# Attention's softmax sums spread over partitions through DRAM, in place of a transpose and selector matmuls, for six of eight groups

## The chip, the core and the metric

The kernel runs on one core of a Trainium2 chip. The core has five engines that run their own instruction streams: TensorE (PE, matrix products; PEld is its weight load), VectorE (DVE), ScalarE (ACT), GpSimd (POOL) and SyncE (SP). In this kernel SP issues almost all DMA transfers, one after the other in one stream. Each engine takes its instructions in order, so an instruction that waits holds up all that stand behind it on that engine. The metric is the device time of one execution in microseconds (us), lower is better.

## The reference

One layer of a hybrid model over 1024 latent tokens (a grid of 16 rows of 64 columns, width 1024) with 256 context tokens: a norm, one projection into an attention part and a state-space part (SSD), both concatenated and projected out, then a gated MLP and a final norm. The change lies in the attention part, cut here to what matters:

```python
# per head (8 heads of 64): local window keys and all context keys in one softmax
scores = jnp.concatenate([s_loc.reshape(bsz, nh, GRID_W, n_loc), s_ctx], axis=-1)
p = jax.nn.softmax(scores.astype(jnp.float32), axis=-1)
out = einsum(p_loc, v_win) + einsum(p_ctx, v_ctx)
```

The softmax is computed as exponentials, their sum for each query and head, the product of the exponentials with v, and last a division of that product by the sum.

## The kernel before, in words

Attention is done in 64 steps (`steps`), one for each head pair `hp` (4), half of the grid's rows `rb` (2), column block `cb` (4) and head of the pair `j` (2). Eight steps with the same `hp` and `rb` are a group; the groups are numbered 0 to 7 here. A step has 128 queries and 640 keys. It goes through three functions, in a software pipeline written out by hand (the loop at L760): `attn_score(n)`, `attn_turn(n - 2)`, `attn_out(n - 3)` (for even steps) and one step of `work`, a generator that first carries the SSD chunks (`ssd_chunk`) and then the first half of the output projection (`out_steps`).

- `attn_score`: scores into PSUM (tile s, tag "big", three buffers of two banks), VectorE subtracts from the bias table `tabt` and takes the extreme (L627), ScalarE takes the exponential and adds it up along the keys into one column of `sm` (L628). So after eight steps `sm` is a tile of 128 queries (partitions) by 8 columns, one for each `cb` and `j`. This function also issues the loads of the next bias table half (`load_tab`, L597), of the next group's q and k (`load_qk`, L544 to L548) and of v (L583).
- `attn_turn`: five transposes of the exponentials (tile pt), copied to SBUF by ScalarE (pts, L639).
- `attn_out`: 20 matmul instructions into `av` (L655), a PSUM tile of one bank with one buffer, that holds for a whole group the output channels of two heads (128 partitions) by 512 queries.

The sums lie with the queries on partitions, and `av` has the queries along the row and the two heads' channels on partitions. So at the end of a group (n % 8 == 6) the reciprocals of the sums must be turned and spread over 64 partitions for each head. The kernel before does this on TensorE: a transpose of `sm` to 8 x 128 (L661, tile smt), a copy (L663, tile st), and four matmuls with selector matrices `selh` (L666, tile rp, eight instructions in the trace) that leave the reciprocals spread over 128 x 512 in PSUM. ScalarE copies them to `ao` (L671), VectorE multiplies `av` by `ao` into `ao` (L672). smt and rp share the PSUM tag "s1" (one bank, one buffer) with the SSD chunks' tiles cb, st, yd and later with ytp and the output projection's os and oa. Groups 0 to 4 are then stored to `a_d` in DRAM (L677) and read back later; groups 5 to 7 are split into two parts for the projection at once (`split_attn`, L684 and L685).

The order of instructions on each engine comes from a scheduler that looks at the code's order and at its own estimate of when each is ready; the code's order is a priority, not the order on the engine.

Of the SSD chunk, the loads `seg<-cum_d` (L439) are of interest: each spreads eight rows of 128 numbers over all 128 partitions by a DMA from DRAM. POOL waits for them at L440, VectorE behind POOL at L443, ScalarE behind VectorE at L444.

Of the kernel before, what the change touches and what calls it, by code (L numbers as in the profile page):

```python
# [10 lines left out]
FP = mybir.dt.float32  # L11
FR = mybir.dt.float32r
AF = mybir.ActivationFunctionType
OP = mybir.AluOpType
# [3 lines left out]
P = 128  # L18
# [18 lines left out]
def hymba(ctx: ExitStack, tc: tile.TileContext, A):  # L37
    nc = tc.nc
    act, dve, pool, pe, sp = nc.scalar, nc.vector, nc.gpsimd, nc.tensor, nc.sync

    const = ctx.enter_context(tc.tile_pool(name="const", bufs=1))
    dram = ctx.enter_context(tc.tile_pool(name="dram", bufs=1, space=DRAM))

    def f32(ap):
        return ap.bitcast(FP)
# [11 lines left out]
    mge, mle, mlt, mgt, ident, ones = (cst[:, i, :] for i in range(6))  # L57
# [5 lines left out]
    a_d = dram.tile([512, T], FP, name="a_d")  # L63
    cum_d = dram.tile([P, P], FP, name="cum_d")
    x1_d = dram.tile([P, KT, T], FP, name="x1_d")
    g_d = dram.tile([NF, P, T], FP, name="g_d")

    wpool = ctx.enter_context(tc.tile_pool(name="wpool", bufs=3, reuse_waits="tile"))

# [33 lines left out]
            pe.matmul(rb[:, t * P:e * P], ones, dg[:, t:e], start=True, stop=True)  # L103
        return rb

    # ---------------------------------------------------------------- projections
    pa = ExitStack()
    hx = pa.enter_context(tc.tile_pool(name="hx", reuse_waits="tile", bufs=1))
    pc = ExitStack()
# [10 lines left out]
    with ExitStack() as p0:  # L120
# [60 lines left out]
        for i in range(4):  # L181
# [10 lines left out]
            for h in range(2):  # L192
                if i == 0 and h:
                    rstd_rows(mmp, wk0, stats(wk0, xh[1], 4, "x1"), 4, "mm", "x1", "sqa4", rb=rbx[1])
                for kt in (2 * i, 2 * i + 1):
                    c = slice(512 * h, 512 * h + 512)
# [32 lines left out]
    with ExitStack() as p1:  # L229
# [40 lines left out]
        for blk in range(4):  # L270
# [3 lines left out]
            g = blk % 2  # L274
# [12 lines left out]
            s = 0.125 if isq else 1.0  # L287
# [35 lines left out]
    sd = ExitStack()  # L323
    ssd = sd.enter_context(tc.tile_pool(name="ssd", reuse_waits="tile", bufs=1, side="right"))
    dtp = sd.enter_context(tc.tile_pool(name="dtp", reuse_waits="tile", bufs=1, side="right"))
    # dt, decays and cumulative sums, tokens on partitions
    dtv = dtp.tile([P, 10, 16], FP, name="dtv")
    dta = dtp.tile([P, 10, 16], FP, name="dta")
    dtt = ExitStack()
# [239 lines left out]

    pa.close()  # L570

    # ---------------------------------------------------------------- attention and SSD
    pb = ExitStack()
    at = pb.enter_context(tc.tile_pool(name="at", reuse_waits="tile", bufs=2))
    bigp = pb.enter_context(tc.tile_pool(name="bigp", reuse_waits="tile", bufs=3, space=PSUM))
    onep = pb.enter_context(tc.tile_pool(name="onep", reuse_waits="tile", bufs=1, space=PSUM))
# [9 lines left out]
    selh = at.tile([8, 4, P], FP, name="selh", bufs=1)  # L586
# [16 lines left out]
    live = {}  # L603
# [40 lines left out]
    def attn_out(n):  # L644
        hp, rb, cb, _ = steps[n]
        vp = vps[hp]
        if n % 8 == 0:
            av_t[0] = onep.tile([P, 4, P], FP, tag="av", name=f"av{n}")
        av = av_t[0]
        pp = [live.pop(n), live.pop(n + 1)]  # L650
        for i in range(5):
            for j in range(2):
                key = i - 2 * j
                vt = vp[:, 4 * cb + rb + key if 0 <= key < 3 else 16 + (i - 3 if key > 2 else i), 64 * j:64 * j + 64]
                pe.matmul(av[64 * j:64 * j + 64, cb], vt, pp[j][:, i * P:(i + 1) * P],  # L655
                          start=i == 0, stop=i == 4, skip_group_check=True)
        if n % 8 == 6:
            sm = live.pop(("sums", n // 8))
            dve.reciprocal(sm, sm)
            sp_ = onep.tile([8, P], FP, tag="s1", name=f"smt{n}")  # L660
            pe.transpose(sp_, sm, ident)  # L661
            st = at.tile([8, P], FP, tag="st", name=f"st{n}", bufs=1)
            dve.tensor_copy(st, sp_)  # L663
            rp = onep.tile([P, 4, P], FP, tag="s1", name=f"rp{n}")
            for cb in range(4):
                pe.matmul(rp[:, cb], selh[:, cb], st,  # L666
                          start=True, stop=True)
            ao = at.tile([P, 8, 4, 16], FP, tag="ao", name=f"ao{n}", bufs=1)
            g4 = lambda ap: ap.rearrange("p b (r c) -> p b r c", r=8)
            av4 = ao.rearrange("p r b c -> p b r c")  # L670
            act.activation(av4, g4(rp), AF.Copy)  # L671
            dve.tensor_tensor(av4, g4(av), av4, OP.mult)  # L672
            ao = ao.rearrange("p r b c -> p (r b c)")
            if (0, rb) in out:
                split_attn(rb, hp, ao)
            else:
                sp.dma_start(a_d[hp * P:(hp + 1) * P, 512 * rb:512 * rb + 512], ao)  # L677
                out["stored"].append((rb, hp))

    out = {"stored": []}  # L680

    def split_attn(hf_, k, src):
        h, l = (o[:, k] for o in out[0, hf_])
        act.activation(h, src, AF.Copy)  # L684
        dve.tensor_tensor(l, src, f32(h), OP.subtract)  # L685
# [74 lines left out]
    for n in range(len(steps) + 3):  # L760
        out["n"] = n
        if n < 64:
            attn_score(n)
        if 0 <= n - 2 < 64:
            attn_turn(n - 2)
        if 0 <= n - 3 < 64 and (n - 3) % 2 == 0:
            attn_out(n - 3)
        next(work, None)
# [1 line left out]
        pass  # L770
    pb.close()

    # ---------------------------------------------------------------- output projection, second half
    psp = ctx.enter_context(tc.tile_pool(name="psp", reuse_waits="tile", bufs=8, space=PSUM))

    def bank(name, n=512):
# [19 lines left out]
            for o, i in ((4, 0), (4, 2), (5, 0), (5, 2), (6, 0), (6, 2), (3, 2))]  # L796
    yzf = yz.rearrange("p a b -> p (a b)")

    # the gated MLP's first product in seven block products of half the size (Strassen)
    ORDER = ((0, 4), (1, 1), (2, 2), (3, 0), (4, 3), (5, 0), (6, 3))  # L800

    B_SUMS = (((0, 0),), ((1, 0), (0, 0), OP.subtract), ((1, 1),), ((0, 0), (1, 1), OP.add),
# [96 lines left out]
    def norm2(hf_, which):  # L899
        c = slice(512 * hf_, 512 * hf_ + 512)  # L900
        rb = rms_rows((ssum[hf_],), wk, f"f{hf_}", yz[:, 0].rearrange("p (n t) -> p n t", n=4))
        yield
        rb = rb()
        for kt in range(KT):
            dve.scalar_tensor_tensor(xa[:, kt, c], xa[:, kt, c], scl[:, 2, kt:kt + 1], rb, OP.mult, OP.mult)
            act.activation(xa[:, kt, c], xa[:, kt, c], AF.Identity, bias=mod[:, 24 + kt:25 + kt])
            if kt % 2:
                yield
        for o in which:
            b_ops(hf_, (o,))  # L910
            yield

    attn_in(1)
    first = norm2(0, range(5))
# [11 lines left out]
    b_ops(0, (5, 6))  # L926
    second = norm2(1, range(7))

    # ---------------------------------------------------------------- gated MLP
    def g_load(hf_, k):  # L930
        h, l = gslots[k - 8]
        sp.dma_start(f32(l), g_d[k, :, 512 * hf_:512 * hf_ + 512])
        act.activation(h, f32(l), AF.Copy)
        dve.tensor_tensor(l, f32(l), f32(h), OP.subtract)
# [3 lines left out]
    for n, u in enumerate(passes):  # L938
        last = n + 1 == len(passes)
        bk = [bank(f"u{n}_{i}") for i in range(5)]  # L940
        r = [xa[:, (4 if units[u][1] else 0) + i] for i in range(2)]
        for o, t0, t1 in (parts[0], parts[0][:6] + parts[1][:6] + whole[6:], parts[1])[n] if n < 3 else whole:
            j = ORDER[o][1]
# [18 lines left out]
        if n == 2:  # L962
            finish(0, [xa[:, i] for i in range(2)])
            u, r = 1, [xa[:, 4 + i] for i in range(2)]
# [2 lines left out]
    g_load(0, 20)  # L967
    g_load(0, 21)

    # ---------------------------------------------------------------- down projection and final norm  # L970
    # of its 22 blocks along the sum, 8 go by the same seven block products and 14 directly
    mt4 = yz[:, 4:6].rearrange("p a (b t) -> p (a b) t", b=2)
    m1, m4, m5, m45 = (mt4[:, i] for i in range(4))
    srow = [yz[:, 6], ssum[1]]
# [62 lines left out]
    for hf_ in range(2):  # L1037
        c = slice(512 * hf_, 512 * hf_ + 512)
# [5 lines left out]
        for p in range(KT // 2):  # L1044
            first = hf_ == 1 and p == 3
# [9 lines left out]
            for i in range(2):  # L1055
                f = 2 * p + i
# [104 lines left out]
```

## Time and profile before

| what | value |
|---|---|
| timed runs | 1433.61, 1435.97 and 1436.22 us; median 1435.97 us |
| the profiled execution, first to last instruction (its span) | 1432.0 us |
| median of the timed runs above that span | 4.0 us |
| instructions in the profile | 19634 |
| TensorE busy | 1344.9 us, 94% of the span |
| VectorE, ScalarE, GpSimd busy | 955.2 us (67%), 598.9 us (42%), 583.6 us (41%) |
| attention's stretch | about 395 to 645 us |

The profiled execution's own time is known from its first to its last instruction, 1432.0 us; what lies before and after is not in the trace. Busy time is when an engine works on an instruction; the busy time of TensorE is modelled for pipelined matmuls, so close to full means that it rarely stands still, not that it is at its peak.

### The profile page before, as it was taken

Reading aid. Unit: us, or ns where it says so; the run is one execution under the profiler, and the core shown is the slowest. Engines: PE = TensorE matmul, PEld = TensorE weight load, DVE = VectorE, ACT = ScalarE, POOL = GpSimd, SP = SyncE. Lnnn points to the kernel's source line nnn. Section 1 sums busy time; section 2 is a strip of 40 time slices with the busy share of each in tenths; the row PEclk is TensorE's granted clock in tenths of the full one; section 3 lists DMA queues with packets and bytes.
Section 4 is the critical chain, followed back from the end, with each engine's and each line's share of the span. In section 5 each row is a group of like instructions: output and inputs, shape, how many; then the busy total and the mean of one; then the engine's idle time right before and its main releaser. Section 6 shows DMA issues by size and latency. Waiting matters only on the chain.

```text
span 1432.0 us, 19634 instructions
## 1 busy us (share of the span) xinstructions
PE 1344.9 (94%) x7539; PEld 1126.8 (79%) x7539; DVE 955.2 (67%) x1251; ACT 598.9 (42%) x987; POOL 583.6 (41%) x389
## 2 busy tenths in 40 slices
PE   5999899999989998999889999999999989998996
PEld 3788888889868787778777777777778767887885
DVE  5797434232367766548989777777787796488574
ACT  5432124342155558535535333344343443354331
POOL 0020000013657852014565676666676554334250
PEclk8999999999989999999989999999999999999998
DMA  9578862021697787343213222212222464364342
GB/s 372 213 238 233 245 228 77 30 74 38 181 253 204 208 222 256 100 153 111 74 48 115 74 89 74 60 73 88 89 88 89 134 224 140 107 199 125 107 141 74
DMA packets 86909, 202.23 MB, mean 141 GB/s; under 512 B 8472, under 2 KB 33816, under 8 KB 85536
## 3 DMA queue, kind: packets, MB, share of 16 engines
q1 hardware_dynamic: 83648, 189.45, 42.3%
q0 software_dynamic: 3168, 11.54, 2.0%
q8 instruction: 59, 0.97, 0.3%
q14 instruction: 34, 0.28, 0.1%
HBM read 163.40 MB, written 37.55 MB: 140 GB/s over the span
## 4 chain that ended last, share of the span: by engine, by line
PE 65%; DVE 15%; DMA 8%; issue 4%; ACT 3%; POOL 3%; SPq 2%; DVEq 0%; ACTq 0%; POOLq 0%
PE u L856 23%; PE pd L88 8%; PE fu_x L88 6%; PE pm L1010 3%; PE av L655 2%; PE tu_z L88 2%; PE oc L88 2%; PE tu_v L88 2%; DMA adal<-in_ada_wt 2%; PE os L88 2%; DMA seg<-cum_d 2%; PE pt L637 2%; PE oa L88 2%; PE s L616 1%; DVE wlu L849 1%
## 5 line engine op out<-in xcount | busy, mean ns | idle before, releaser
L856 PE MATMUL u<-op,whu 128*128 128x512 f32 (+1 forms) x760 | 229.7, 386 | 5.9 <-ACT whu L848 2.5
L856 PEld LDWEIGHTS u<-op,whu 128*128 128x128 f32 x760 | 141.9, 192 | 38.0 <-ACT whu L848 2.7
L856 PE MATMUL u<-op,wlu 128*128 128x512 f32 (+1 forms) x380 | 145.9, 385 | 2.2 <-DVE wlu L849 2.2
L849 DVE TENSOR_TENSOR wlu<-yz,whu 128x512 fp32r<-128x512 f32 x115 | 135.9, 1196 | 17.5 <-ACT whu L848 16.8
L847 POOL TENSOR_TENSOR yz<-as,as 128x512 f32<-128x512 f32 x69 | 118.9, 1735 | 46.7 <-DVE wlu L849 45.8
L848 ACT ACTIVATE whu<-yz 128x512 fp32r<-128x512 f32 x115 | 70.9, 626 | 116.1 <-PE u L856 68.0
L856 PE MATMUL u<-opx,whu 128*128 128x512 f32 (+1 forms) x384 | 113.1, 383 | 3.5 <-ACT whu L848 3.5
L395 POOL TENSOR_TENSOR xwc<-ctm,wendc 128x512 f32<-128x512 f32 x4 | 4.7, 1166 | 218.6 <-PE fu_c L88 200.9
L847 POOL TENSOR_TENSOR yz<-as 128x512 f32<-128x512 f32 x46 | 64.0, 1400 | 62.1 <-DVE wlu L849 52.4
L856 PEld LDWEIGHTS u<-opx,whu 128*128 128x128 f32 x384 | 69.6, 191 | 22.2 <-ACT whu L848 8.9
L856 PEld LDWEIGHTS u<-op,wlu 128*128 128x128 f32 x380 | 73.0, 192 | 17.6 <-DVE wlu L849 2.6
L88 PE MATMUL pd<-opx,wh_dn 128*128 128x512 f32 x256 | 80.6, 398 | 3.7 <-ACT wh_dn L77 3.7
L856 PE MATMUL u<-opx,wlu 128*128 128x512 f32 (+1 forms) x192 | 72.7, 380 | 0.0
L887 POOL TENSOR_TENSOR xa<-xa 128x1024 f32<-128x1024 f32 x20 | 51.7, 2586 | 45.6 <-DVE xa L877 45.4
L628 ACT ACTIVATE pr<-pr,mx 128x640 f32<-128x640 f32 x64 | 52.8, 826 | 40.5 <-DVE mx L627 40.4
L627 DVE CUSTOM_DVE_ANT_0 pr<-s,tabt 128x640 f32<-128x640 f32 x64 | 52.0, 818 | 20.6 <-PE s L617 15.8
L849 DVE TENSOR_TENSOR wlu<-as,whu 128x512 fp32r<-128x512 f32 x46 | 46.2, 1004 | 26.0 <-ACT whu L848 26.0
L655 PE MATMUL av<-pts,vp 128*64 128x128 f32 x640 | 56.4, 289 | 5.5 <-ACT pts L639 4.9
L208 DVE CUSTOM_DVE_ANT_0 adal<-adal,crow 128x1024 f32<-128x1024 f32 x32 | 39.6, 1240 | 30.8 <-DMA adal<-in_ada_wt 30.8
L88 PEld LDWEIGHTS pd<-opx,wh_dn 128*128 128x128 f32 x256 | 47.5, 188 | 16.0 <-ACT wh_dn L77 4.8
L856 PE MATMUL u<-opz,whu 128*128 128x512 f32 (+1 forms) x192 | 57.4, 381 | 0.6 <-DVE opz L816 0.6
L639 ACT ACTIVATE pts<-pt 128x640 f32<-128x640 f32 x64 | 43.8, 696 | 32.2 <-PE pt L637 20.3
(660 smaller groups left out, 3785.5 us busy)
## 6 DMA issues: line engine op xcount, KB each, us to landing
as<-in_w_up SPq DMA_DIRECT2D x46, 512.0 KB, 4.2
adal<-in_ada_wt SPq DMA_DIRECT2D x32, 512.0 KB, 4.7
ws_dn<-in_w_down SPq DMA_DIRECT2D x32, 448.0 KB, 3.5
g_d<-xa POOLq DMA_DIRECT2D x22, 512.0 KB, 4.5
tabt<-in_tab SPq DMA_DIRECT2D x48, 192.0 KB, 4.4
adaw<-in_ada_w SPq DMA_DIRECT2D x8, 1024.0 KB, 12.2
seg<-cum_d SPq DMA_DIRECT2D x16, 512.0 KB, 5.5
q<-q_d SPq DMA_DIRECT2D x32, 256.0 KB, 6.5
```

What stands on the lines that cost most here:

```text
L88: pe.matmul(out[:, t0:t1], st(a, k), mv(b, k, t0, t1), start=k == 0 and p == 0, stop=k == kend - 1 and p == 2, **kw)
L208: dve.tensor_tensor_reduce(w, w, crow, 1.0, 0.0, OP.mult, OP.add, modr[:, f - 16:f - 15])
L627: dve.tensor_tensor_reduce(pr, ps[:, lo:lo + 640], tabt[m % 2][:, 384 * j:384 * j + 640], -1.0, BIG, OP.add, OP.min, mx)
L628: act.activation(pr, pr, AF.Exp, bias=mx, scale=-1.0, accum_out=sm[:, n % 8:n % 8 + 1])
L639: act.activation(pts, pt[:, 0:640], AF.Copy)
L655: pe.matmul(av[64 * j:64 * j + 64, cb], vt, pp[j][:, i * P:(i + 1) * P], start=i == 0, stop=i == 4, skip_group_check=True)
L847: pool.tensor_tensor(src, e[0], e[1], e[2])
L848: act.activation(h, src, AF.Copy)
L849: dve.tensor_tensor(l, src, f32(h), OP.subtract)
L856: pe.matmul(ps[:, t0:t1], aops[n, o][a][:, k], bops[o][b][:, k, t0:t1], start=first and o < 5 and (t0 == 0 or n == 2), stop=end, skip_grou ...
L887: (dve if p == 0 else pool).tensor_tensor(r[i], r[i], tmp, OP.mult)
L1010: pe.matmul(dst[o], aops[n, o][a][:, k], sops[o][b][:, k], start=k == i == 0 and (o in (0, 2, 4) or o > 4 and first), stop=k == 3 and i == ...
```

## The change

For groups 0 to 5 the reciprocals go to DRAM and come back spread. A DRAM tensor `s_d` (6 x 8 x 128) is added. At the end of such a group SP stores `sm` (128 partitions of 8 numbers) into it turned, so that each of the 8 columns becomes a row of 128; in DRAM neighbouring numbers of one partition then lie 512 bytes apart. Two loads follow, one for each head of the pair, that read four rows of 128 numbers and repeat them over 64 partitions, into a new SBUF tile `rows` (128 x 512, one buffer). ScalarE copies `av` itself from PSUM to `ao`. The product of `ao` and `rows` on VectorE (`normalised`) is written later in the code: after the next group's first 20 `av` matmuls. What follows the product (the store to `a_d`, or the split) moves with it. Groups 6 and 7 keep the old way. The rest of the diff only takes away comments.

```diff
+    s_d = dram.tile([6, 8, P], FP, name="s_d")
...
+        if n % 8 == 0 and "rows" in live:
+            normalised(*live.pop("rows"))
         if n % 8 == 6:
-            sm = live.pop(("sums", n // 8))
+            g = n // 8
+            sm = live.pop(("sums", g))
             dve.reciprocal(sm, sm)
-            sp_ = onep.tile([8, P], FP, tag="s1", name=f"smt{n}")
-            pe.transpose(sp_, sm, ident)
-            st = at.tile([8, P], FP, tag="st", name=f"st{n}", bufs=1)
-            dve.tensor_copy(st, sp_)
-            rp = onep.tile([P, 4, P], FP, tag="s1", name=f"rp{n}")
-            for cb in range(4):
-                pe.matmul(rp[:, cb], selh[:, cb], st,
-                          start=True, stop=True)
             ao = at.tile([P, 8, 4, 16], FP, tag="ao", name=f"ao{n}", bufs=1)
-            g4 = lambda ap: ap.rearrange("p b (r c) -> p b r c", r=8)
             av4 = ao.rearrange("p r b c -> p b r c")
-            act.activation(av4, g4(rp), AF.Copy)
-            dve.tensor_tensor(av4, g4(av), av4, OP.mult)
...
+            if g < 6:
+                rows = at.tile([P, 4, P], FP, tag="rows", name=f"rows{n}", bufs=1)
+                sp.dma_start(s_d[g].rearrange("k q -> q k"), sm)
+                for j in range(2):
+                    src = s_d[g].rearrange("(b j) q -> j b q", j=2)[j]
+                    sp.dma_start(rows[64 * j:64 * j + 64], src.partition_broadcast(64))
+                act.activation(av4, g4(av), AF.Copy)
+                live["rows"] = (ao, rows, hp, rb)
             else:
...
+                act.activation(av4, g4(rp), AF.Copy)
+                dve.tensor_tensor(av4, g4(av), av4, OP.mult)
+                attn_done(ao, hp, rb)
...
+    def normalised(ao, rows, hp, rb):
+        av4 = ao.rearrange("p r b c -> p b r c")
+        dve.tensor_tensor(av4, av4, g4(rows), OP.mult)
+        attn_done(ao, hp, rb)
+
+    def attn_done(ao, hp, rb):
+        ao = ao.rearrange("p r b c -> p (r b c)")
+        if (0, rb) in out:
+            split_attn(rb, hp, ao)
+        else:
+            sp.dma_start(a_d[hp * P:(hp + 1) * P, 512 * rb:512 * rb + 512], ao)
+            out["stored"].append((rb, hp))
```

## Rows read from the trace of the kernel before

**Rows 1.** The page: busy time, share of the span, instructions of each engine.
```profile
PE 1344.9 (94%) x7539; PEld 1126.8 (79%) x7539; DVE 955.2 (67%) x1251; ACT 598.9 (42%) x987; POOL 583.6 (41%) x389
```

**Rows 2.** Attention's stretch: length, engines' busy time, granted clock, DMA share, GB/s.
```profile
395.00:645.00 250.00, 235.13 (x1715) 195.19 (x1716) 161.62 (x275) 140.02 (x259) 113.27 (x75) 0.96 0.67 199
```

**Rows 3.** Groups of instructions, 395 to 645 us: busy, mean ns | idle before, releasers.
```profile
L655 PE MATMUL av<-pts,vp 128*64 128x128 f32 x640 | 56.4, 289 | 5.5 <-ACT pts L639 4.9 <-DVE ao L672 0.5
...
L666 PE MATMUL rp<-st,selh 8*128 8x128 f32 x64 | 10.1, 302 | 0.1
...
L661 PE MATMUL smt<-cst,sm 128*8 128x128 f32 x8 | 2.3, 290 | 0.2 <-DVE yn L715 0.2
...
L627 DVE CUSTOM_DVE_ANT_0 pr<-s,tabt 128x640 f32<-128x640 f32 x64 | 52.0, 818 | 20.6 <-PE s L617 15.8 <-DMA tabt<-in_tab 3.2 <-ACT pts L639 0.7
...
L672 DVE TENSOR_TENSOR ao<-av,ao 128x512 f32<-128x512 f32 x7 | 4.8, 690 | 9.8 <-ACT ao L671 6.1 <-ACT pr L628 3.7
```

**Rows 4.** The chain of waits, 395 to 650 us: start, length, what.
```profile
402.81 7.80 DMA seg<-cum_d
...
427.41 1.08 PE rp L666 x8
...
502.65 2.00 PE rp L666 x8
...
560.87 1.08 PE rp L666 x8
```

**Rows 5.** From each reciprocal to the next group's first products, groups 0 to 5 (columns as rows 2).
```profile
420.40:433.70 13.30, 13.20 (x87) 11.13 (x87) 9.51 (x19) 7.52 (x16) 9.10 (x6) 0.77 0.47 153
445.20:459.00 13.80, 13.59 (x110) 11.80 (x111) 8.65 (x18) 6.98 (x14) 9.12 (x7) 1.00 1.06 304
467.30:483.60 16.30, 15.79 (x141) 13.81 (x141) 11.44 (x22) 9.51 (x19) 11.61 (x8) 1.00 0.61 227
493.70:514.00 20.30, 18.32 (x126) 15.39 (x126) 13.58 (x23) 9.02 (x17) 11.59 (x8) 0.83 1.02 246
526.30:540.00 13.70, 13.31 (x111) 11.48 (x111) 8.15 (x16) 7.88 (x16) 5.12 (x4) 1.00 0.52 121
549.30:569.50 20.20, 18.57 (x164) 15.10 (x161) 14.73 (x32) 15.48 (x31) 6.81 (x6) 1.00 0.81 250
```

**Rows 6.** DMA queues of 383 to 395 us: packets, MB, share of 16 engines.
```profile
DMA packets 3675, 3.28 MB, mean 273 GB/s; under 512 B 148, under 2 KB 3179, under 8 KB 3674
...
q1 hardware_dynamic: 3674, 3.27, 99.0%
```

**Rows 7.** DMA queues and issues of the whole span; issues: KB each, us to landing.
```profile
q1 hardware_dynamic: 83648, 189.45, 42.3%
...
cum_d<-cts SPq DMA_DIRECT2D x1, 64.0 KB, 1.5
```

**Rows 8.** Bias table loads (L597) in 420 to 430, 445 to 455 and 493 to 508 us.
```profile
DMA to landing us min/median/max: 2.3/2.3/2.3
...
DMA to landing us min/median/max: 5.9/5.9/5.9
...
DMA to landing us min/median/max: 9.7/9.8/9.9
```

**Rows 9.** SP: a store's time of issue (ns min/median/max), and its longest wait, 395 to 650 us.
```profile
L677 SPq DMA_DIRECT2D a_d<-ao x5: 326/382/3885, 430.9 to 533.8; - x5
...
SPq L597 <- DVE mx L627: 29.0, 20, 4.4
```

**Rows 10.** Timeline, groups 1 and 3, reciprocal and product: start, us, instruction [idle before <-releaser].
```profile
445.19 0.19 DVE L659 RECIPROCAL sm<-sm 128x8 f32<-128x8 f32 x1
...
451.55 0.69 DVE L672 TENSOR_TENSOR ao<-av,ao 128x512 f32<-128x512 f32 x1 [0.94 <-ACT ao L671]
...
493.72 0.20 DVE L659 RECIPROCAL sm<-sm 128x8 f32<-128x8 f32 x1
...
507.07 0.69 DVE L672 TENSOR_TENSOR ao<-av,ao 128x512 f32<-128x512 f32 x1 [3.73 <-ACT pr L628]
```

More of the change, by code (lines that the diff above doesn't have):

```diff
@@ L673, in attn_out @@
-            ao = ao.rearrange("p r b c -> p (r b c)")
-            if (0, rb) in out:
-                split_attn(rb, hp, ao)
-            else:
-                sp.dma_start(a_d[hp * P:(hp + 1) * P, 512 * rb:512 * rb + 512], ao)
-                out["stored"].append((rb, hp))
+            if g < 6:
[6 more added lines that the diff above has]
+                live["rows"] = (ao, rows, hp, rb)
+            else:
+                sp_ = onep.tile([8, P], FP, tag="s1", name=f"smt{n}")
+                pe.transpose(sp_, sm, ident)
+                st = at.tile([8, P], FP, tag="st", name=f"st{n}", bufs=1)
+                dve.tensor_copy(st, sp_)
+                rp = onep.tile([P, 4, P], FP, tag="s1", name=f"rp{n}")
+                for cb in range(4):
+                    pe.matmul(rp[:, cb], selh[:, cb], st,
+                              start=True, stop=True)
+                act.activation(av4, g4(rp), AF.Copy)
+                dve.tensor_tensor(av4, g4(av), av4, OP.mult)
+                attn_done(ao, hp, rb)
@@ new lines, in hymba @@
+    g4 = lambda ap: ap.rearrange("p b (r c) -> p b r c", r=8)
+    def normalised(ao, rows, hp, rb):
[9 more added lines that the diff above has]
+            out["stored"].append((rb, hp))
```

## The prediction

> **What bounds the kernel now.** I read the page first. TensorE is busy for 94% of the span, the next engine for 67% [rows 1], so a saving counts if it shortens TensorE's stream or what TensorE waits for. But the change touches only attention's stretch, so I read that by itself: in 250 us TensorE is busy for 235.1 and stands still for 14.9, VectorE is busy for 161.6, ScalarE for 140.0, and the 16 DMA engines for 0.67 of the time [rows 2]. That is the picture to keep: TensorE nearly full, VectorE with a third to spare, DMA two thirds used. A step takes 250 / 64 = 3.9 us.
>
> Third, the groups of instructions [rows 3]. TensorE hardly waits for the part that is removed: before rp 0.1 us, before smt 0.2, before av for the product that frees it 0.5. The long wait is VectorE's: 9.8 us before seven products `ao`. VectorE before the extreme L627 mostly waits for scores (15.8 us), so it runs a little ahead of what TensorE gives it. Fourth, the chain of waits through the stretch [rows 4]: it has rp in five of the six groups, and stretches like the 7.8 us for a seg load, where not TensorE but a transfer sets the pace. Last, the six places at which the change acts [rows 5]: there TensorE idles from 0.1 us (group 0) to 2.0 (group 3), the granted clock is 0.77 and 0.83 in two of them (a part of the time at 1.2 instead of 2.4 GHz), and the DMA share is from 0.47 to 1.06. Groups 1, 3 and 5 end where DMA has nothing free.
>
> **The change part by part.**
>
> *Removed from TensorE.* Six of eight rp and smt. By busy time that is 10.1 x 6/8 = 7.6 us and 2.3 x 6/8 = 1.7, together 9.3 [rows 3]: the upper bound, since ends of matmuls overlap. The lower bound is what the chain credits: four pieces of 1.08 us and one of 2.00 at the low clock, 6.3 us; group 2's rp is not on it [rows 4]. I take 8.0, in the middle: TensorE is busy for 235 of 250 us, so nearly all of what it doesn't do lets the next matmul start.
>
> *Removed elsewhere.* Six copies st on VectorE and six uses of the one-buffer tag "s1". The waits that TensorE has for these are under 0.3 us each group of lines [rows 3], so they go at nothing; what covers them is TensorE's own work, and without that cover they would be worth what VectorE waits before the product, 9.8 us for seven. `av` becomes free after ScalarE's copy, no longer after the product: at most the 0.5 us of [rows 3], counted at nothing.
>
> *Changed.* ScalarE's copy reads `av` in place of rp, same shape, nothing. VectorE's product reads two SBUF tiles instead of PSUM and SBUF, 0.69 us each [rows 10]; no row shows that form, and I take it the same.
>
> *Added to SP.* Three DMA issues a group, eighteen in all, about 0.38 us each [rows 9]: 1.1 us a group, in a queue that itself waits 29.0 us in 20 waits for its next bias load to be allowed [rows 9]. Nothing, as long as that slack stands.
>
> *Added to DMA.* The store writes 1024 runs of 4 bytes, 64 on each of 16 engines; the loads write 2 x 256 runs of 512 bytes, 32 on each. No row shows 4-byte runs. The nearest: in 383 to 395 us, 3674 packets of mostly under 2 KB filled 99.0% of 16 engines for 12 us, 0.99 x 12 x 16 / 3674 = 0.052 us a packet [rows 6]. From above: the mean packet of the whole run, 0.423 x 1432 x 16 / 83648 = 0.116 us [rows 7]. From below nothing, if such small runs cost nearly nothing. I take 0.052, the row with the smaller packets: store 64 x 0.052 = 3.3 us, loads 32 x 0.052 = 1.7, together 5.0 us of all 16 engines a group, 30 for six (0 to 67). What of it reaches TensorE? In the whole stretch DMA is busy for 0.67 x 250 = 168 us and TensorE idles for 14.9, so at most 0.09 us idle for each us of DMA. That gives 2.7 us (0 to 6.0).
>
> The Trainium skill speaks against this store (DMA: Bandwidth & Descriptors, "Rules for kernel authors"): a last dimension that is not contiguous becomes one descriptor for each element, and one should rearrange until it is contiguous. By that rule the store is 1024 descriptors for 4 KB. No transfer in this trace has such a form, so no run here yet shows its price; what it would do is the fourth rival below.
>
> *The new wait.* The product now stands behind store, landing, two loads, landing. Free of traffic: issue 0.4, store 3.3 + 1.5 (the landing of the small cum_d store [rows 7]), two issues 0.8, a landing of 2.3 (the bias load near group 0 [rows 8]): 8.3 us after the reciprocal. In traffic I take the landing that bias loads had there, twice: group 1 5.9, group 3 9.8 [rows 8], so 0.4 + 5.9 + 0.8 + 5.9 = 13.0 and 20.8 us. In the code the product comes after the next group's first av. In the trace that is 13.3, 13.8, 16.3, 20.3, 13.7 and 20.2 us after the reciprocal (the windows are cut so, [rows 5]). So rows come just in time almost everywhere, if VectorE keeps the code's order: late by 0.5 us in group 3, early by 0.8 in group 1. Behind a product that waits stand the extremes L627 of the next steps, and behind them exponentials, transposes and av. But the order is not the code's; products in the old trace came 6.4 us (group 1) and 13.4 us (group 3) after the reciprocal [rows 10]. Kept in those places they would wait 6.6 and 7.4 us, 14 together: the upper bound; the lower is nothing. I take 3.2 us, what the bias loads, transfers that the extremes wait for directly, cost VectorE in the whole stretch [rows 3], and half of that, 1.6, for TensorE, since VectorE has a third of its time free.
>
> *Also held: SP.* The two loads wait on SP for the store's landing, and bias, seg, q and k loads stand behind them. This is costed at nothing: q and k are loaded a group ahead, and bias loads are held by VectorE's extremes anyway. If that cover goes, it is the second rival.
>
> *Sum.* -8.0 + 2.7 + 1.6 = -3.7 us. Against the profiled execution that is a span of 1428.3; with the 4.0 us that the median lies above the span, 1432.3 us.
>
> **The rivals.** A difference under 0.2%, 2.9 us, is about what a measurement of this kernel can't tell from none.
>
> 1. *More than the sum.* Group 3 loses (1 - 0.83) x 20.3 = 3.5 us to the low clock [rows 5], and VectorE there waits 3.7 us for the old product [rows 10]. If without that wait the clock stays up: -3.7 - 3.5 = -7.2, 1428.8 us, and the 2.0 us idle beside it would make 1426.8. Against: the spell begins where seg loads are late, and they stay.
>
> 2. *No change, since SP pays.* SP is held 5.9 and 9.8 us for the store in groups 1 and 3 [rows 8]. Its longest slack before a bias load is 4.4 us [rows 9]; beyond that bias and seg loads are late by 1.5 + 5.4 = 6.9 us. All of it on TensorE gives -8.0 + 2.7 + 6.9 = +1.6, 1437.6 us; half gives -1.8, 1434.1. For it: seg loads set the chain in places [rows 4]. Against: VectorE waited only once for a bias load.
>
> 3. *Slower, since VectorE is held.* The scheduler places the products as early as before, and they wait 14 us in groups 1 and 3: -8.0 + 2.7 + 14 = +8.7, 1444.7 us. It decides from 8.2 us of hold that reach TensorE (8.0 - 2.7 + 2.9), so 60% of the 14. For it: these two places have a DMA share over 1.0. Against: VectorE already waited 9.8 us for products, and TensorE lost 0.5 to that.
>
> 4. *Slower, since the store is dear.* At 0.116 us a run, store and loads fill all DMA engines for 96 x 0.116 = 11.1 us a group; in groups 1, 3 and 5, which have nothing free, all loads are later by that, 33 us. If half reaches TensorE: -8.0 + 16.7 = +8.7, 1444.7 us.
>
> That the change doesn't remove the matmuls can't be: the code of groups 0 to 5 has none left.
>
> **How the numbers follow.** Chances: the sum's case, 1428 to 1433 us, 0.50; rival 1, 0.07; rival 2 with its neighbours within 2.9 us, 0.25; rival 3, 0.12; rival 4, 0.06. Faster 0.57, same 0.25, slower 0.18. The predicted time is the sum's, 1432.3. The range goes from rival 1's end, 1426.5, to the middle between rival 2 and the slow ones, 1441: outside lie about 0.03 below and 0.10 above. A further unknown is in all cases: the scheduler's order of the whole stretch may change by the removal, which is worth some us to either side and is why the range isn't narrower.
>
> **What would show it.** Right: in the stretch, rp 16 and smt 2 instructions, TensorE's busy time lower by about 8 us and its idle time not more than 4 us higher; av no longer waits for the product. The store's landing should be near 5 us in quiet places. Rival 2 shows as SP's wait for the store with bias or seg loads behind, and VectorE's L627 waiting for tabt; rival 3 as idle before the product that ends with the DMA of rows, over 8 us in all; rival 4 as a landing of the store beyond 9 us and a DMA share that rises by more than 0.2 in the stretch; rival 1 as a granted clock near 1.0 in group 3's place. Wrong would be: TensorE's busy time doesn't fall, or its idle time grows by as much.

## The result, and the profile after

The changed kernel takes 1468.23 us (median of 4 runs, 1466.67 to 1472.70) beside 1434.9 us for the kernel before (1433.61 to 1436.22): a ratio of 1.0244, 95% interval 1.0218 to 1.0269. The prediction was 1432.3 us and "faster" at 0.57; the result is slower by 33 us and lies far outside the range. The profiled execution took 1469.35 us with a span of 1467.6.

First the page: busy time by engine, then the DMA packets. They answer to [rows 1].

```profile
PE 1343.4 (92%) x7485; PEld 1122.3 (76%) x7485; DVE 951.9 (65%) x1245; ACT 598.0 (41%) x987; POOL 582.3 (40%) x389
...
DMA packets 96414, 203.83 MB, mean 139 GB/s; under 512 B 14904, under 2 KB 43320, under 8 KB 95040
```

No engine works more than before, and TensorE has 54 instructions less. So the 35.6 us by which the span grew are waiting (and some low clock), not added work.

Where? The gated MLP's first product, u, follows attention. Its first instruction, in the kernel before and after (duration ns, first and last start):

```profile
L856 PE MATMUL u<-opx,whu x74: 277/282/415, 696.7 to 758.9; 128*128 128x256 f32 x64, 128*128 128x512 f32 x10
```

```profile
L878 PE MATMUL u<-opx,whu x32: 278/281/300, 732.2 to 750.5; 128*128 128x256 f32 x32
```

It starts 35.5 us later, so practically the whole loss is in attention's stretch. The windows from 395 us to that start, before and then after (columns as in [rows 2]), say in what form:

```profile
395.00:696.70 301.70, 284.05 (x1914) 233.96 (x1915) 205.47 (x316) 165.47 (x293) 138.93 (x84) 0.95 0.60 182
```

```profile
395.00:732.20 337.20, 286.22 (x1861) 233.41 (x1862) 199.98 (x307) 164.14 (x293) 137.91 (x84) 0.92 0.62 166
```

TensorE stood still for 301.70 - 284.05 = 17.7 us before and stands still for 51.0 now: 33.3 us more. Its busy time is 2.2 us higher although 9.6 us of matmuls are gone (below): the granted clock fell from 0.95 to 0.92 of full speed, and the 640 matmuls of av took 295 ns each in place of 289. The sign of being wrong that the prediction named, an idle time that grows by as much as it hoped to save, is there four times over. The DMA share hardly rose (0.60 to 0.62).

The groups of instructions of the change, 380 to 690 us after (they answer to [rows 3]):

```profile
L628 DVE CUSTOM_DVE_ANT_0 pr<-s,tabt 128x640 f32<-128x640 f32 x64 | 52.0, 817 | 24.7 <-PE s L618 13.1 <-DMA tabt<-in_tab 9.8 <-issue 1.0
...
L691 DVE TENSOR_TENSOR ao<-ao,rows 128x512 f32<-128x512 f32 x6 | 4.3, 719 | 41.9 <-DMA rows<-s_d 41.9
...
L681 PE MATMUL rp<-st,selh 8*128 8x128 f32 x16 | 2.3, 283 | 0.5 <-DVE st L678 0.4
...
L676 PE MATMUL smt<-cst,sm 128*8 128x128 f32 x2 | 0.5, 272 | 0.8 <-DVE xa L716 0.8
```

The matmuls are gone as the diff says: rp 10.1 to 2.3 us, smt 2.3 to 0.5, together 9.6. But VectorE stands for 41.9 us before its six products (before: 9.8 us for seven, [rows 3]). The waits of 380 to 690 us (engine, line and what it waited for: us, times, longest) show three queues held:

```profile
ACT pr L629 <- DVE mx L628: 67.1, 25, 14.0
...
DVE ao L691 <- DMA rows<-s_d: 41.9, 6, 11.6
POOL seg L441 <- DMA seg<-cum_d: 40.2, 8, 12.9
...
PE pt L638 <- DVE mx L628: 20.3, 8, 5.7
...
PE yd L465 <- DVE mt L454: 10.0, 2, 8.7
...
PE s L617 <- DVE mx L628: 8.5, 1, 8.5
```

The same waits of ScalarE and POOL in the kernel before:

```profile
ACT pr L628 <- DVE mx L627: 40.4, 28, 7.5
...
POOL seg L440 <- DMA seg<-cum_d: 23.4, 10, 9.8
```

The last three lines of the first list are where TensorE lost its time: it waits 38.8 us for VectorE there, and in the kernel before, in the same three places, 2.2 (0.9, 0.0 and 1.3).

SP is held too (its own waits, 395 to 690 us), and the store's landing heads it (DMA issues of that stretch: KB, median us to landing):

```profile
SPq L671 <- DMA s_d<-sm: 44.7, 6, 10.1
```

```profile
rows<-s_d SPq DMA_DIRECT2D x12, 128.0 KB, 3.3
...
s_d<-sm SPq DMA_DIRECT2D x6, 4.0 KB, 11.2
```

The 4 KB take 11.2 us, a load of 128 KB behind them 3.3. Group 3 shows this in the open. SP, then VectorE and TensorE, from the timeline (start, us, instruction, idle before it):

```profile
520.51 0.38 SPq L668 DMA_DIRECT2D s_d<-sm  x1
523.65 0.33 SPq L598 DMA_DIRECT2D tabt<-in_tab  x1
534.13 1.24 SPq L671 DMA_DIRECT2D rows<-s_d  x2
...
538.25 0.69 DVE L691 TENSOR_TENSOR ao<-ao,rows 128x512 f32<-128x512 f32 x1 [11.56 <-DMA rows<-s_d]
538.87 1.22 DVE L454 TENSOR_TENSOR mt<-mt,seg 128x1024 f32<-128x1024 f32 x1
...
540.14 2.18 PE L465 MATMUL yd<-xtm,mt 128*128 128x64 f32 x9 [8.75 <-DVE mt L454]
```

Read it upwards: TensorE idles 8.75 us for mt, mt stands behind the product, the product idles 11.56 us for rows, the loads of rows wait for the store, and the store took 13.6 us to land. And in 527 to 534 us the DMA engines did almost nothing (packets, MB; queue's share of 16 engines):

```profile
DMA packets 7, 0.01 MB, mean 1 GB/s; under 512 B 1, under 2 KB 7, under 8 KB 7
...
q1 hardware_dynamic: 7, 0.01, 2.3%
```

In the 6.5 us ahead of that, 520.5 to 527, the same view has 1152 packets under 512 B, which is room for all 1024 of the store, and nearly all of them lie in 1.5 us, 524.5 to 526:

```profile
DMA packets 1352, 0.37 MB, mean 250 GB/s; under 512 B 1081, under 2 KB 1350, under 8 KB 1351
...
q1 hardware_dynamic: 1351, 0.36, 105.1%
```

So the store isn't waiting for a turn: its packets have been taken, and it lands some 8 us later. Nor are its packets dear: those 1351 took 1.051 x 1.5 x 16 / 1351 = 0.019 us each in the mean, larger ones included. The bias load issued at 523.65 landed 10.6 us after its issue, at 534.2, just behind the store.

### The profile page after: what moved, and what is told of

Its sections match the earlier page's. It is cut to its first block, busy times and chain, and to the rows that moved or that the text cites. A ratio compares the mean times of both kernels' runs of the same rounds, so it can differ in the third digit from the quotient of the medians.

```text
span 1467.6 us, 19564 instructions
## 1 busy us (share of the span) xinstructions
PE 1343.4 (92%) x7485; PEld 1122.3 (76%) x7485; DVE 951.9 (65%) x1245; ACT 598.0 (41%) x987; POOL 582.3 (40%) x389
## 4 chain that ended last, share of the span: by engine, by line
PE 41%; DVE 10%; DMA 5%; issue 3%; ACT 2%; POOL 1%; SPq 0%; DVEq 0%; ACTq 0%; POOLq 0%
PE u L878 22%; PE pd L89 8%; PE pm L1032 3%; PE os L89 2%; PE oa L89 2%; DVE wlu L871 1%; PE oc L89 1%; DVE op L1013 1%; PE pd L1032 1%; DMA xa<-g_d 1%; DVE op L838 1%; DMA as<-in_w_up 1%; PE av L656 1%; DMA tabt<-in_tab 1%; DMA q<-q_d 1%
## 5 line engine op out<-in xcount | busy, mean ns | idle before, releaser
L638 PE MATMUL pt<-cst,pr 128*128 128x128 f32 x320 | 50.3, 291 | 24.0 <-DVE mx L628 20.3
L628 DVE CUSTOM_DVE_ANT_0 pr<-s,tabt 128x640 f32<-128x640 f32 x64 | 52.0, 817 | 24.7 <-PE s L618 13.1
L638 PEld LDWEIGHTS pt<-cst,pr 128*128 128x128 f32 x320 | 39.3, 150 | 30.1 <-issue 19.9
L617 PE MATMUL s<-k,q 128*128 128x384 f32 x128 | 50.1, 411 | 11.4 <-DVE mx L628 8.5
```

Source lines behind the costliest of these rows:

```text
L617: pe.matmul(ps[:, loc0:loc0 + 384], qs, kl, start=a == 0, stop=a == 1)
L628: dve.tensor_tensor_reduce(pr, ps[:, lo:lo + 640], tabt[m % 2][:, 384 * j:384 * j + 640], -1.0, BIG, OP.add, OP.min, mx)
L638: pe.transpose(pt[:, i * P:(i + 1) * P], pr[:, i * P:(i + 1) * P], ident)
```

## The experiments

The theory after the result: the store's 4-byte runs are slow to land, and everything follows from that. The rivals: SP's hold is the cause; VectorE's wait is the cause; or any added traffic. And the first term, TensorE's saving, had to be measured by itself.

**1. The store side by side.** Each partition writes its 8 numbers as one run of 32 bytes.

```diff
-                sp.dma_start(s_d[g].rearrange("k q -> q k"), sm)
+                sp.dma_start(s_d[g].rearrange("k q -> (k q)").rearrange("(q k) -> q k", k=8), sm)
```

> The changed kernel, but the store writes each partition's eight numbers side by side in DRAM (128 runs of 32 bytes in place of 1024 runs of 4); loads and product stay, so the numbers that come back are in another order and groups 0 to 5 are divided by the wrong sums: only the time is read. Theory A (the 4-byte runs make the store land late, and VectorE's product and SP's loads wait for that landing): store lands in 2 to 5 us instead of 9.5 to 13.6, VectorE's wait before the product falls from 41.9 us to under 10, time 1428 to 1440. Theory B (any round trip through DRAM is too long here, whatever its runs): landing stays above 8 us, time 1455 or more.

Measured: 1437.02 us, ratio 1.0031 (1.0012 to 1.0051). Same store of 4 KB, same chain of store, loads and product, and of the 33 us 3.5 are left (1433.56 us for the kernel before beside this one). The store lands after 6.4 us (median; 3.6 to 7.2) in place of 11.2. VectorE still waits 13.4 us for rows, in three groups of six. The time is theory A's; landing and wait are both above what it expected:

```profile
L671 SPq DMA_DIRECT2D rows<-s_d x12: 579/594/1318, 422.3 to 565.9; - x12
...
  DVE ao L691: 13.4, 3
```

**2. No transfer at all.** Groups 0 to 5 multiply by a tile of ones; neither store nor loads, and the matmuls stay out.

```diff
-                rows = at.tile([P, 4, P], FP, tag="rows", name=f"rows{n}", bufs=1)
-                sp.dma_start(s_d[g].rearrange("k q -> q k"), sm)
...
+                rows = rows1
```

> The changed kernel without store and loads: rows is a tile of ones, so groups 0 to 5 aren't divided by their sums. All that is taken from TensorE stays taken. It shows what the removed matmuls are worth. Theories A and B, and the prediction's first term: 8 us less than before, 1424 to 1430. Theory C (the new order of instructions itself is bad, whatever the transfers): above 1440.

Measured: 1433.57 us, ratio 0.9989 (0.9975 to 1.0004). This is the best that the change could have given with its order of instructions, and it misses the 1424 to 1430 expected. u starts at 693.7 us, 3.0 earlier than before; the rest of the 9 us of removed matmuls isn't found, and the span of the profiled execution, 1433.3 us, is no shorter than before. POOL waits 29.5 us for seg loads (23.4 in the kernel before, 380 to 690 us in both).

**3. The kernel before with the transfers added.** The matmuls stay; store and loads are issued, and nobody reads rows. (A1 is the rival that VectorE's wait is the cause, A2 that SP's hold is.)

```diff
+                sp.dma_start(s_d[g].rearrange("k q -> q k"), sm)
+                for j in range(2):
+                    src = s_d[g].rearrange("(b j) q -> j b q", j=2)[j]
+                    sp.dma_start(rows[64 * j:64 * j + 64], src.partition_broadcast(64))
```

> The kernel before with the store and the two loads of the six groups added, and nobody reads what they load: the old path through TensorE computes. It shows the price of the transfers and of SP's hold without VectorE's. Theory A1: 1434 to 1445. Theory A2: 1455 or more.

Measured: 1469.36 us, ratio 1.0254 (1.0229 to 1.0279). As slow as the change, though no product on VectorE waits for rows. POOL waits 55.6 us for seg loads (23.4 before), and VectorE waits behind POOL. SP waits 30.5 us for the store. So a product that waits for rows isn't needed for the loss.

**4. The product late.** The changed kernel, its product placed four steps later and behind the next group's last extreme L628, with ao's one buffer (two don't fit into SBUF beside the rest) and groups 0 to 4 stored to a_d.

```diff
-        if n % 8 == 0 and "rows" in live:
+        if n % 8 == 4 and "rows" in live:
...
+        with tc.issue_after(live["ext"]):
+            dve.tensor_tensor(av4, av4, g4(rows), OP.mult)
```

> The changed kernel with the product of each of the six groups put behind the next group's last extreme on VectorE, so that rows have long landed. Store, loads and SP's wait for the store stay where they were. Theory A1 (VectorE held by the product costs the 33 us): wait before the product under 3 us in all, time 1428 to 1440. Theory A2 (SP held by the store's landing costs it, bias and seg loads come late): the time stays above 1455, though the product doesn't wait, and VectorE still waits some 10 us for bias loads. In between, 1440 to 1455: both have a part.

Measured: 1461.91 us, ratio 1.0194 (1.0147 to 1.0241). VectorE's wait for rows is gone, but POOL's for seg loads is 60.1 us and SP's for the store 30.7. The time is theory A2's, its sign isn't: VectorE waits 2.5 us for bias loads where some 10 were expected; it is the seg loads that come late. So most of the loss doesn't need the product's wait. How much that wait adds in the change this run can't say: the two intervals (this and 1.0218 to 1.0269) overlap, and the late product has a cost of its own, 5.4 us that TensorE waits for ScalarE's copy to ao.

**5. The store alone.** The kernel before, with the store and nothing else; no instruction reads what it writes.

```diff
+                sp.dma_start(s_d[g].rearrange("k q -> q k"), sm)
```

> The kernel before with the six stores of 4-byte runs added and no loads, so that nothing on SP waits for the store's landing. Theory A2 (SP's wait is what costs): 1433 to 1439, no more than 3 us above the kernel before; the store still lands in 9 us or more. Theory D (the 4-byte runs themselves hold up the other transfers in the DMA rings): 1455 or more, and loads issued behind the store land several us later than in the kernel before.

Measured: 1461.73 us, ratio 1.0202 (1.0163 to 1.0240). This is the main result: six stores of 4 KB that nobody reads cost 29 us (the trace puts one wait down to them, 1.4 us of SP). POOL's wait for seg loads doubles, from 23.4 to 48.8 us (380 to 690 us):

```profile
POOL seg L441 <- DMA seg<-cum_d: 48.8, 10, 9.0
```

The DMA issues and q1 of 395 to 645 us, in this kernel:

```profile
q1 hardware_dynamic: 33397, 45.30, 74.6%
...
seg<-cum_d SPq DMA_DIRECT2D x12, 512.0 KB, 11.5
...
s_d<-sm SPq DMA_DIRECT2D x6, 4.0 KB, 11.6
```

In the kernel before the median seg load lands after 6.1 us. The 11.5 and 11.6 here rest on few transfers: of the twelve seg loads three have a landing on record (4.8, 11.5 and 14.1 us), of the six stores three (9.1, 11.6 and 13.3), so POOL's wait is the firmer sign. SP feels it too: after the second store its timeline has an issue of 11 us where the trace of before has 0.4 (median; 3.9 at most, [rows 9]), as if the queue took no more:

```profile
447.50 0.38 SPq L663 DMA_DIRECT2D s_d<-sm  x1
...
454.04 11.01 SPq L681 DMA_DIRECT2D a_d<-ao  x1
```

**6. The loads late.** The changed kernel with the two loads issued behind a bias load of the next group's last steps and the product two steps after them, so that SP doesn't stand for the store.

```diff
+        if n % 8 == 4 and "loads" in live:
+            g, rows = live.pop("loads")
+            with tc.issue_after(live["tab"]):
...
+        if n % 8 == 6 and "rows" in live:
```

> The changed kernel with the two loads issued on SP behind the bias load of the next group's last step, and the product behind the extreme two steps after that: SP no longer stands before a store that hasn't landed, and VectorE not before rows. All the transfers are still made. Theory A2: SP waits under 5 us for the store in all (44.7 in the changed kernel), time 1429 to 1437, about that of the kernel without transfers (1433.6). Theory D: above 1450.

Measured: 1467.11 us, ratio 1.0226 (1.0192 to 1.0260). SP's wait for the store falls from 44.7 to 6.9 us (three waits, 3.0 at most; under 5 was expected), and the time doesn't fall. But the late product keeps ao's only buffer, and TensorE waits 23.1 us in four places for ScalarE's copy behind it, a cost of this kernel's own. So this run suggests that the loss doesn't need SP's hold, as 5 shows; how much the hold costs in the change it can't say.

**7 to 9. The same store with gaps.** As in 5, but in DRAM the numbers lie 64, 16 or 32 bytes apart (here 16): the same 1024 runs of 4 bytes.

```diff
-    s_d = dram.tile([6, 8, P], FP, name="s_d")
+    s_d = dram.tile([6, 8, P, 4], FP, name="s_d")
...
-                sp.dma_start(s_d[g].rearrange("k q -> q k"), sm)
+                sp.dma_start(s_d[g, :, :, 0].rearrange("k q -> q k"), sm)
```

> As the kernel before with the store only, but each 4-byte run goes to a 64-byte block of DRAM of its own (a tensor 16 times as large), where the changed kernel writes 128 runs side by side. Theory E (runs that fall next to each other in DRAM wait for each other): the store lands in under 6 us. Theory F (each run of 4 bytes has its price wherever it goes): it lands in 9 us or more, as there.

> As the kernel before with the store only, each 4-byte run 16 bytes from the next in DRAM, so four fall into a 64-byte block (16 at the changed kernel's stride of 4 bytes, one at 64 bytes). Theory E (runs in one block follow each other, blocks go side by side): between the two, time 1434 to 1445, landing 4 to 8 us. Theory F (the number of runs alone counts): contradicted already by the stride of 64.

> The same with a stride of 32 bytes, two runs in a 64-byte block. Theory E with blocks of 64 bytes: a little above the stride of 64 bytes, 1433 to 1437. If the block is 32 bytes or smaller: as the stride of 64 bytes.

Measured, one run each: 1433.26 us at 64 bytes, 1431.84 at 32, 1428.69 at 16, where the kernel before had medians of 1433.01 and 1434.13. With gaps the store costs nothing that one run can show, against 29 us without. And the DMA engines handle as many packets of every size: the pages of 5 and of the kernel with 16 bytes have

```profile
DMA packets 93149, 202.25 MB, mean 139 GB/s; under 512 B 14712, under 2 KB 40056, under 8 KB 91776
```

```profile
DMA packets 93149, 202.25 MB, mean 142 GB/s; under 512 B 14712, under 2 KB 40056, under 8 KB 91776
```

(the kernel before has 8472 under 512 B, so each store adds 1040). Only the addresses in DRAM differ. The rows that answer to those of 5, for 16 bytes:

```profile
q1 hardware_dynamic: 34908, 48.86, 68.1%
...
seg<-cum_d SPq DMA_DIRECT2D x12, 512.0 KB, 6.8
...
s_d<-sm SPq DMA_DIRECT2D x6, 4.0 KB, 6.2
```

The store lands in 6.2 us (4.7 to 11.0), seg loads in 6.8, and q1 is less busy with more bytes. At 32 and 64 bytes the store lands in 7.1 (4.5 to 10.9) and 7.0 (3.5 to 9.6). The longest of each, 11.0, 10.9 and 9.6 us, is group 3's, where bias loads took 9.7 to 9.9 us in the kernel before too [rows 8]. So theory E has the direction, but not its scale: the landing at 64 bytes is above its 6 us, and at 16 bytes the time is below its 1434 to 1445, so no price that grows with the number of runs in 64 bytes shows. The issue of 11 us is 4.6 here. In group 1, where the two kernels issue the same transfers in the same order and at the same distances, the store, seg and z loads land after 6.7, 7.2 (median of two) and 7.8 us with gaps; without, the one seg load of the two whose landing is on record took 11.5 and the z load 14.2. From 5 to 9 us after the issue of that store, when its packets have been taken, q1 shows how (without gaps, then with 16 bytes; packets, MB, share of 16 engines):

```profile
q1 hardware_dynamic: 89, 0.23, 102.2%
```

```profile
q1 hardware_dynamic: 380, 1.13, 89.8%
```

The engines are as full, but a packet of the transfers behind the store takes 1.022 x 4 x 16 / 89 = 0.73 us in place of 0.15, and a fifth of the bytes gets through.

**10 and 11. What the removed matmuls are worth.** The kernel before without its seg loads (POOL makes zeros of the same shape), and experiment 2 without them.

```diff
-            sp.dma_start(sg, cum_d[r0:r0 + 8].partition_broadcast(P))
-            pool.tensor_tensor(sg, sg, cum[:, d, c][:, :, None].to_broadcast([P, 8, P]), OP.subtract)
+            cum8 = cum[:, d, c][:, :, None].to_broadcast([P, 8, P])
+            pool.tensor_tensor(sg, cum8, cum8, OP.subtract)
```

> The kernel before without the sixteen seg loads of the SSD chunks (POOL subtracts the cumulative sums from themselves, so all decays are one): transfers that POOL, VectorE and ScalarE wait for are gone, TensorE's work is the same. To be read against the next one. Theory G (it is those loads, not TensorE, that set the pace at most group ends, so that the removed matmuls gave nothing): 8 to 20 us less than the kernel before, and taking the six groups' matmuls away on top of it gives 5 to 9 us. Theory H (TensorE's wait comes from the pipeline of score, extreme and exponential itself): about the time of the kernel before, and the matmuls are worth under 3 us here too.

> The same without the seg loads, from the kernel without transfers (rows of ones, six groups' rp and smt gone). Theory G: 5 to 9 us less than the previous one. Theory H: less than 3 us less.

Measured: 1422.51 us (0.9910, 0.9878 to 0.9941) and 1416.21 us (0.9868, 0.9832 to 0.9905). The seg loads cost the kernel before some 12 us. Without them the removed matmuls seem worth 6.3 us, against 0 to 3.6 with them (experiment 2's interval). The two intervals overlap, so this points to the loads as what hides the saving, and doesn't settle it.

**12. The whole computation with a store of rows.** TensorE still turns the reciprocals (smt) and VectorE copies them (st). The store then writes eight rows of 512 bytes, and the loads spread them; only the selector matmuls go.

```diff
-                sp.dma_start(s_d[g].rearrange("k q -> q k"), sm)
+                sp_ = onep.tile([8, P], FP, tag="s1", name=f"smt{n}")
+                pe.transpose(sp_, sm, ident)
+                st = at.tile([8, P], FP, tag="st", name=f"st{n}", bufs=1)
+                dve.tensor_copy(st, sp_)
+                sp.dma_start(s_d[g], st)
```

> This kernel computes the whole reference: for groups 0 to 5 TensorE still turns the reciprocals (smt, VectorE's copy st), then st is stored to s_d as eight rows of 512 bytes and read back by the same two broadcast loads; only the selector matmuls rp go. Theory, the loss comes from the 4-byte runs that lie side by side in DRAM, and the removed matmuls are mostly hidden behind the seg loads: the store lands in 3 to 7 us (9 to 13.6 us with the 4-byte runs), VectorE waits for rows under 20 us in all, seg loads cost POOL about what they cost in the kernel with the contiguous store (31 us), and the time is 1433 to 1439 us, no faster than the kernel before. Rival, any store that SP's loads have to wait for costs this much: VectorE still waits near 40 us for rows and the time is over 1455 us. Second rival, the removed matmuls do pay once the store is cheap: 1426 to 1430 us.

Measured: 1433.48 us (12 runs), ratio 0.9998 (0.9984 to 1.0011). The whole loss is gone, and no gain takes its place, with 48 matmuls fewer than in the kernel before. The landing of this store is not on record. SP's and VectorE's waits for the same chain are now (395 to 650 us; and who waited for s_d's loads):

```profile
SPq L675 <- DMA s_d<-st: 8.8, 5, 4.2
```

```profile
  DVE ao L695: 2.4, 3
```

44.7 us of SP became 8.8, and 41.9 us of VectorE 2.4. Not all of this is the form of the store: SP now stands 12.0 us for the copy st ahead of it. The form alone, in 1, brought SP to 17.9 and VectorE to 13.4.

## Why the prediction was wrong, point by point

**The step that failed most: the landing of the store,** costed as 64 packets at 0.052 us plus the 1.5 us of cum_d's landing, 4.8 us, and in traffic as a bias load's landing, 5.9 us in group 1 and 9.8 in group 3. It took 9.5 to 13.6 us in the six groups, 11.3 and 13.6 in those two, with the engines idle for the last 7 us in group 3. Of its two parts the packets were costed too high (0.019 us in the mean in group 3, larger ones included), and what follows them far too low: 1.5 us against some 8 in group 3. The row for the packets has other sizes, and the 1.5 us is the landing of a store in another form. No row of before had short runs side by side. The prediction said so, and its bounds covered engine time only, not landing.

**What reaches TensorE from DMA, 2.7 us (0 to 6.0),** failed in kind. It turned busy time of the DMA engines into idle time of TensorE at 0.09. From 395 us to u's start the DMA engines were busy for 0.60 x 301.7 = 181 us before and 0.62 x 337.2 = 209 after, 28 more where 30 were forecast. That is luck: the store's packets are shorter than costed, and it is the packets behind such a store that take long (with gaps of 16 bytes the sum is 0.62 x 300.4 = 186). TensorE stood still for 33.3 us more, not 2.7, since transfers that others wait for were held (5 against 7 to 9, 29 us from the store alone).

**The removed matmuls, -8.0 us (6.3 to 9.3).** They left the stream as said, 9.6 us of busy time in the trace. Without any price they bring 0 to 3.6 us (experiment 2). The reason given, that TensorE is busy for 235 of 250 us so that what it doesn't do moves the next matmul forward, doesn't hold where seg loads set the pace, as 10 and 11 suggest. The chain in [rows 4] already showed these loads; the prediction saw them, used them for rival 2, and didn't take them off this term.

**The wait of the product, 1.6 us for TensorE (VectorE 3.2, at most 14).** VectorE waited 41.9 us in all six groups. Two things were wrong. Rows were there late: the product started 14.0, 19.3, 16.7, 19.0, 15.3 and 21.9 us after its reciprocal, where 8.3 was reckoned in quiet and 13.0 in group 1. (In group 3 the reckoning, 20.8, was no shorter than what came.) And VectorE came to the product early: taking off the idle time before it, 7.1, 9.8, 12.1, 7.4, 6.7 and 21.1 us after the reciprocal, not the 13.3 to 20.3 read off TensorE's av. The code's order was kept, but VectorE runs ahead of TensorE by steps, so TensorE's windows were the wrong clock for it. TensorE's waits in the changed kernel end with VectorE, but this wait isn't needed for the loss: 3 is as slow without it.

**SP's hold, costed at nothing.** SP waited 44.7 us for the store, and seg loads stood behind it. From 5 (1.0202) to 3 (1.0254) the loads and this hold are added: some 7 us, with intervals that overlap. It is a second part of the loss at most. The two ways of paying also replace each other: where SP stands until the store has landed, the seg load behind it is issued late and then lands in the usual time (median 6.5 us in the change, 6.1 before); where SP doesn't stand, as in 5, it is held in the queue.

**Smaller slips.** Group 5 was counted among those with nothing free in DMA; its share is 0.81 [rows 5]. And the 4.0 us added for what lies outside the span are in good part the spread of the runs: where both numbers are on record the difference is 1.8 (1469.35 and 1467.6).

**The rivals.** Signs of three of them show at once: SP's wait (2), VectorE's idle time before the product (3), a landing beyond 9 us (4). Number 4 came nearest to the cause, at a chance of 0.06, and its price (0.116 us a run, paid as a DMA share higher by more than 0.2; it rose by 0.04 in 395 to 645 us) was the wrong mechanism. The rule beside it in the Trainium skill (DMA: Bandwidth & Descriptors, "Rules for kernel authors": one descriptor for each element if the last dimension isn't contiguous) was right against this store, and 12 follows its advice. The trace agrees on the count: six stores add 6240 packets under 512 B to the page, 1040 each for 1024 elements. But the count isn't the price: with gaps of 16 bytes the page has as many packets, and no loss shows.

**What is behind the slow landing** is open in part. Shown: among these stores only the one of neighbouring 4-byte runs has it. Gaps of 16, 32 and 64 bytes remove it (one run each, all three near the kernel before), and so do runs of 32 bytes side by side; gaps of 8 bytes are open. The smallness of a run alone isn't it, since the runs with gaps are as small, nor the small area, since the 32-byte runs fill the same 4 KB. Neighbours in DRAM come from different partitions here; whether that matters, and why side by side is slow, stays open.

That other transfers are held has a rule in the Trainium skill (DMA: Bandwidth & Descriptors, "Queues, rings and completion order"): the write that signals the end of a transfer comes only after all earlier writes of that DMA engine. The trace agrees in group 3, where the bias load landed 0.2 us behind the store with the engines idle for 7 us. It would explain why a store that nobody reads delays loads. But it can't be all: in group 1 of 5 the packets behind the store take 0.73 us each in place of 0.15, so the data itself is held there, and not only its signal. No run took that order away, so its part is argued, not shown.

## What to carry to other kernels

Before sending a small tile through DRAM, look at how its runs lie there: 1024 numbers written side by side, 4 bytes each, cost 5 us a store here though nobody read them, while the same numbers 16 bytes apart, or in rows of 512 bytes, cost nothing measurable. Price a transfer by its landing and by what lands behind it in the same queues, not by its bytes or the busy share of the DMA engines. And a matmul saved is worth its time only where TensorE, not a load, sets the pace: leave out everything that the change adds and measure that best case first.

## What the runs showed of the hardware

- Six stores of 4 KB in neighbouring 4-byte runs slow a kernel of 1433 us by 2.0% (1.6 to 2.4) though no instruction reads them; median landing 11.6 us (three on record; 11.2 of six in the changed kernel), against 6.2, 7.1 and 7.0 us of six at 16, 32 and 64 bytes apart, with the same number of packets.
- Behind such a store packets of other transfers took 0.73 us in the mean (89 in 4 us), behind the one with gaps of 16 bytes 0.15 (380 in 4 us).
- A landing can lag its packets by 7 us: 7 packets in 527 to 534 us, store and bias load landing at 534.1 and 534.2.
- Behind such a store an issue on SP can take 11.0 us (4.5 to 5.4 with gaps).
